# A hand-written order for the merge loop of a hybrid DiT block, with its sums on VectorE, and earlier sums in the first items of the up projection

## The chip, the cores and the metric

The kernel runs on one core of a Trainium2 chip. A core has five engines with queues of their own: TensorE (PE in the profile; its weight loads are shown apart as PEld), VectorE (DVE), ScalarE (ACT), GpSimd (POOL) and SyncE (SP), which here issues the loads and stores. Each engine works its own queue strictly in order; semaphores hold an instruction back until what it reads is there or what it overwrites has been read. The metric is the device time of one execution in microseconds.

## The reference

One layer on 1024 tokens of 1024 channels (batch 1), in fp32:

```python
attn = banded_window_attention(q, k, v, kc, vc, sink[l])
y = merge_branches(attn, fourier_mix(f), g_a, g_f, w_pa[l], w_pf[l], w_out[l])
x = x + gt1 * rmsnorm(y, g_post1[l])
h2 = modulate(rmsnorm(x, g_pre2[l]), sh2, sc2)
x = x + gt2 * rmsnorm(conv_ffn(h2, w_up[l], conv_w[l], conv_b[l], w_down[l]), g_post2[l])

def merge_branches(attn_o, four_o, g_a, g_f, w_pa, w_pf, w_out):
    m = jax.nn.sigmoid(g_a) * (attn_o @ w_pa) + jax.nn.sigmoid(g_f) * (four_o @ w_pf)
    return m @ w_out

def conv_ffn(h, w_up, conv_w, conv_b, w_down):
    u, gate = jnp.split(h @ w_up, 2, axis=-1)
    up = jnp.pad(u, ((0, 0), (1, 1), (0, 0)))
    u = up[:, :-2] * conv_w[0] + up[:, 1:-1] * conv_w[1] + up[:, 2:] * conv_w[2] + conv_b
    return (jax.nn.silu(u) * gate) @ w_down
```

## The kernel before

**Number format.** Each fp32 matrix is kept as two rounded parts, a high one (`h`, a cast on ScalarE, L80) and a low one (`l`, the value minus the high part, a subtraction at L68, which is the one line for all element-wise sums). A product is three matmuls, high·high, high·low, low·high, on three lines (L85, L86, L87; `mm3`).

**Merge.** The merged map is transposed, channels on partitions: 16 tiles of 128 channels (j = 0 to 7) by 512 tokens (h = 0, 1). A tile is 12 matmuls (4 K parts of 3) of `w_pa` (high `whpa`, low `wlpa`) with the attention's output (`ah`, `al`) into a PSUM bank `pa`; then `sga`, the gate's half, is multiplied by `pa` on DVE, `mf`, the Fourier half, gets `sga` added on POOL, and the sum is split into `mh` (ACT) and `ml` (DVE). The first two tiles are computed at the end of the attention (`EARLY`), the other 14 in a loop. The same loop loads and splits the four later blocks of `w_pa` (raw `wpa`; low part on POOL) and the 16 blocks of `w_out` (raw `wor`; parts `w0a`, `w0b` for the left half of the output channels, `woh` and `wol` for the right half; `wo_load`). Before the change this loop is plain code whose order on the engines is set by an automatic scheduler; in what follows it in the program, from the output map to the end, the order is the order of the code (`tc.manual_schedule()`). The tiles `sga` and `mf` of the sixth loop tile and later, and after them the rows `xr` of the residual, come from a pool `so` with 11 buffers that are handed on in order of allocation. The 8 DMA queue semaphores are used in turn, so each load of SP waits until the load eight before it has landed.

**Output map.** For 8 blocks of 128 tokens and two halves of the output channels, `y_mm(tk, h)` is 8 K parts of 3 matmuls, `mh` and `ml` being stationary. Then comes a token's chain: squares (`jy`, ACT), norm (a dozen small DVE operations, one square root on ACT), gate and residual (`z`, `xr`, DVE), squares, norm, scale (`z`), eight transposes on PE (`y_turn`, `ptz`, L160) and an affine step into `h` (`y_affine`, DVE and ACT).

**First items of the up projection.** It is a 2x2 Strassen product with seven products P1 to P7 for each of the row blocks j. Stationary operands are made from four blocks of `w_up` (`A_u`): A11, A12, A22 themselves and the sums S1 = A21+A22, S3 = A11−A21, S2 = S1−A11, S4 = A12−S2; each is then split (`conv`: `hP_u` on ACT, `lP_u` on DVE). Moving operands are made from `h`: B11, B21, B22 and T1, T2, T3, T4n, which are differences of quarters of the tokens (`t1` to `t4`), split by `hb_puts` (four casts of three quarters `a` and of one quarter `b` on ACT, and as many subtractions on DVE). The first items run in the order P1 (j = 0, 1, 2; `mm(0)` to `mm(2)`), P2 (j = 0, 1), P5 on T1 (`mm(5)` to `mm(7)`), P6 on T2 (`mm(8)` to `mm(10)`), P7 on T3 (`mm(11)` to `mm(13)`), then P4 of j = 0 on T4n (`mm(14)`) and P3 on B22; each is 12 matmuls. `evac` copies a bank to `snP_u` or adds it to a copy. From `run(14, M)` on, a planner goes through the items.

Of the kernel before, what the change touches and what calls it, by code (L numbers as in the profile page):

```python
# [16 lines left out]
P = 128  # L17
# [23 lines left out]
def block_kernel(ctx: ExitStack, tc: tile.TileContext, t: dict, out: bass.AP, dbg: dict):  # L41
# [169 lines left out]
    def wino(pairs, items, psf, hooks, slots=False, seng=None):  # L211
# [60 lines left out]
        def rest(j):  # L272
            if "P1" in st[j] and "S3" in st[j]:
                do_add(j, "S2")
                if "P2" in st[j]:
                    do_add(j, "S4")
# [1229 lines left out]
    for i in range(EARLY):  # L1506
        pa_tile(*PA[i], psB.tile([P, 1024], F, tag="ss", name=f"pa{i}", bufs=2)[:, :512])
# [27 lines left out]
    def wo_load(k, h):  # L1535
# [352 lines left out]
    with tc.manual_schedule():  # L1888
# [13 lines left out]

        def y_new(tk):
# [5 lines left out]

        xr_load(0)  # L1910
        for tk in range(6):
            xr_load(tk + 1)
            if tk:
                x1_store(tk - 1)
            if 1 <= tk < 4:
                pre(tk - 1, ("A11", "A21"))
            if 2 <= tk < 4:
                pre(tk - 2, ("A22",))
            y_mm(tk, 0)
            y_square(tk, 0)  # L1920
            y_mm(tk, 1, range(6))
            if tk:
                y_turn(tk - 1)
            y_mm(tk, 1, range(6, KT))
            if tk:
                y_affine(tk - 1, range(4), V)
                y_affine(tk - 1, range(4, 8), None)
# [8 lines left out]
            if 2 <= tk < 4:  # L1936
# [25 lines left out]
        pre(2, ("A12", "A22"))  # L1962
# [183 lines left out]
```

## Time and profile before

| | |
|---|---|
| Runs | 1362.89, 1367.26, 1368.34 us; median 1367.26 |
| Profiled execution | 1363.15 us; span 1361.4; granted clock 0.98 |
| Busy share of the span | PE 94%, PEld 76%, DVE 75%, ACT 51%, POOL 33% |
| DMA | 219.42 MB, mean 161 GB/s |
| Last matmul of the attention to the end of the first three tokens' output map | 528.85 to 614.97 us |
| Start of the up projection on PE | 672.94 us |

How to read it: in the trace PE is a single line of matmuls, so time is lost only where PE is idle or runs at a reduced clock. The profile's rows give a start, a duration, the engine, the line, the operation, the tiles and in brackets the idle time before with what ended it. The windows view gives, for a stretch of time, how long each engine was busy in it, and the clock that TensorE was granted (PEclk, 1.00 is full).

### The profile page before, as it was taken

To read this page: it belongs to the slowest core of one execution; us is meant where nothing else is said; L and a number is where in the kernel's file an instruction comes from. 1 tells how busy PE (TensorE), PEld (TensorE's weight loads), DVE (VectorE), ACT (ScalarE), POOL (GpSimd) and SP (SyncE) were. 2 spreads that over 40 slices of the span, in tenths; PEclk is the share of its full clock that TensorE was granted. 3 is DMA by queue.
4 is the path that set the end of the run, shared out by engine and by line. 5 is a ranking of instruction groups with operands and counts; after the bars stand their busy time and mean duration, and the time that the engine had idled before them with its cause. 6 is when DMAs were issued, how large, how long until landed. Compare 5 with 4: busy or idle time off the path is not lost.

```text
span 1361.4 us, 18457 instructions
## 1 busy us (share of the span) xinstructions
PE 1278.7 (94%) x5976; PEld 1031.9 (76%) x5976; DVE 1026.6 (75%) x1807; ACT 690.9 (51%) x1421; POOL 446.3 (33%) x337
## 2 busy tenths in 40 slices
PE   5889999999999999989989999999999988999896
PEld 3458777887878877778768788888888876878774
DVE  4787676974888985856689987766676687796987
ACT  5685346533667774434457554444454444543442
POOL 0000221200343343500004544454344355372764
PEclk9999999999999999899989999999999999999998
DMA  9986284614233436833203564444434559946563
GB/s 308 362 285 194 94 263 138 190 32 150 62 109 118 123 117 199 285 97 122 78 16 93 161 168 136 131 132 116 124 106 121 169 166 292 302 142 223 184 214 124
DMA packets 251125, 219.42 MB, mean 161 GB/s; under 512 B 14973, under 2 KB 204053, under 8 KB 251029
## 3 DMA queue, kind: packets, MB, share of 16 engines
q1 hardware_dynamic: 251028, 218.25, 52.2%
q8 instruction: 47, 0.77, 0.2%
q14 instruction: 50, 0.40, 0.1%
HBM read 159.20 MB, written 58.72 MB: 160 GB/s over the span
## 4 chain that ended last, share of the span: by engine, by line
PE 66%; DVE 14%; DMA 7%; issue 4%; ACT 3%; POOL 2%; SPq 2%; DVEq 0%; POOLq 0%; ACTq 0%
PE X_u L86 5%; PE X_u L87 5%; PE X_u L85 5%; PE Y_u L85 3%; PE Y_u L86 3%; PE Y_u L87 2%; PE y L87 2%; PE X_d L85 2%; PE y L85 2%; PE y L86 2%; DVE p L1285 2%; PE X_g L85 2%; PE X_d L87 2%; DVE pl L68 2%; PE X_d L86 2%
## 5 line engine op out<-in xcount | busy, mean ns | idle before, releaser
L68 DVE TENSOR_TENSOR lP_u<-A_u,hP_u 128x512 fp32r<-128x512 f32 x132 | 101.7, 779 | 48.3 <-ACT hP_u L303 46.5
L365 ACT COPY snP_u<-X_u 128x512 f32<-128x512 f32 x57 | 33.5, 588 | 138.2 <-PE X_u L87 130.4
L1305 POOL TENSOR_SCALAR p<-p,sm 128x640 f32<-128x640 f32 (+1 forms) x64 | 48.5, 778 | 84.3 <-PE po L1321 30.1
L68 POOL TENSOR_TENSOR yd<-yd,snP_d 128x512 f32<-128x512 f32 x36 | 52.2, 1451 | 70.2 <-ACT snP_d L365 70.2
L303 ACT CAST hP_u<-A_u 128x512 fp32r<-128x512 f32 x121 | 74.5, 619 | 0.1
L68 POOL TENSOR_TENSOR A_u<-A_u,A_u 128x512 f32<-128x512 f32 x39 | 62.9, 1613 | 34.3 <-DVE lP_u L68 21.0
L365 ACT COPY snP_d<-X_d 128x512 f32<-128x512 f32 x48 | 28.1, 586 | 78.7 <-PE X_d L87 78.7
L68 POOL TENSOR_TENSOR A_u<-S_u,A_u 128x512 f32<-128x512 f32 x19 | 24.9, 1309 | 104.1 <-DVE lP_u L68 104.1
L80 ACT CAST ph<-pp 128x512 fp32r<-128x512 f32 x76 | 44.3, 585 | 23.0 <-PE pp L1310 21.7
L68 DVE TENSOR_TENSOR pl<-pp,ph 128x512 fp32r<-128x512 f32 x76 | 51.7, 681 | 3.1 <-ACT ph L80 2.6
L1299 ACT ACTIVATE p<-p,nm 128x640 f32<-128x640 f32 (+1 forms) x64 | 51.3, 802 | 0.7 <-DVE nm L1292 0.7
L68 DVE TENSOR_TENSOR lP_d<-rP_d,hP_d 128x384 fp32r<-128x384 f32 x48 | 42.3, 882 | 10.5 <-ACT hP_d L303 10.3
L1285 DVE CUSTOM_DVE_ANT_0 p<-ss,mask 128x640 f32<-128x640 f32 (+1 forms) x64 | 49.9, 781 | 0.0
L1310 PE MATMUL pp<-ident,p 128*128 128x128 f32 x304 | 46.7, 274 | 3.2 <-POOL p L1305 1.8
L68 POOL TENSOR_TENSOR S_u<-A_u,A_u 128x512 f32<-128x512 f32 x19 | 34.5, 1816 | 39.5 <-DVE T4nb L68 38.9
L68 POOL TENSOR_TENSOR shk<-shk,rope 128x512 f32<-128x512 f32 x2 | 3.2, 1621 | 133.4 <-DMA A_g<-in_w_in 127.6
L1310 PEld LDWEIGHTS pp<-ident,p 128*128 128x128 f32 x304 | 37.2, 140 | 12.2 <-POOL p L1305 3.5
L1687 DVE SCALAR_TENSOR_TENSOR tb<-u,vec,tb 128x1024 f32<-128x1024 f32 x22 | 41.1, 1870 | 6.5 <-ACT tb L1684 6.5
L68 DVE TENSOR_TENSOR dB<-wd,dB 128x512 fp32r<-128x512 f32 x33 | 38.9, 1189 | 7.7 <-ACT dB L1758 7.7
L68 POOL TENSOR_TENSOR wd<-wd,wd 128x512 f32<-128x512 f32 x22 | 37.0, 1700 | 20.2 <-DVE dB L68 11.4
L68 DVE TENSOR_TENSOR u<-Y_u,snP_u 128x512 f32<-128x512 f32 x22 | 15.2, 690 | 37.3 <-PE Y_u L87 37.3
L68 POOL TENSOR_TENSOR fl<-fr,fh 128x512 fp32r<-128x512 f32 x6 | 7.6, 1286 | 100.0 <-ACT fh L80 99.1
(896 smaller groups left out, 4584.6 us busy)
## 6 DMA issues: line engine op xcount, KB each, us to landing
A_u<-in_w_up SPq DMA_DIRECT2D x88, 256.0 KB, 3.7
wd<-in_w_down SPq DMA_DIRECT2D x55, 256.0 KB, 4.5
wa<-in_w_mod SPq DMA_DIRECT2D x36, 256.0 KB, 5.3
A_g<-in_w_in SPq DMA_DIRECT2D x32, 256.0 KB, 5.3
ws<-in_w_mod SPq DMA_DIRECT2D x30, 256.0 KB, 6.0
wm<-in_w_mod SPq DMA_DIRECT2D x30, 256.0 KB, 4.6
bP_d<-g_d0P SPq DMA_DIRECT2D x56, 128.0 KB, 3.1
x<-in_x SPq DMA_DIRECT2D x16, 256.0 KB, 6.0
```

The lines of the kernel that those rows point to most:

```text
L68: return (eng or nc.vector).tensor_tensor(out=out, in0=a, in1=b, op=op)
L80: copy(hi, src)
L85: nc.tensor.matmul(ps, ah, bh, start=start, stop=False, skip_group_check=True)
L86: nc.tensor.matmul(ps, ah, bl, start=False, stop=False, skip_group_check=True)
L87: nc.tensor.matmul(ps, al, bh, start=False, stop=stop, skip_group_check=True)
L303: copy(st[j]["half", p][0], st[j][STA[p]])
L365: copy(d["s" + p], d["X"])
L1285: nc.vector.tensor_tensor_reduce(out=p_, in0=ssc[:, lo:768], in1=self.mk, op0=ALU.add, op1=ALU.max, scale=1.0, scalar=-3.0e38, accum_out=s ...
L1299: nc.scalar.activation(out=self.pt[g], in_=self.pt[g], func=AF.Exp, scale=SCALE, bias=self.m[:, g:g + 1], accum_out=self.sm[:, g:g + 1])
L1305: nc.gpsimd.tensor_scalar(out=self.pt[g], in0=self.pt[g], scalar1=self.sm[:, g:g + 1], scalar2=1.0, op0=ALU.mult, op1=ALU.mult)
L1310: nc.tensor.transpose(pp[:, g * P:(g + 1) * P], self.pt[g][:, j * P:(j + 1) * P], ident)
L1687: nc.vector.scalar_tensor_tensor(out=tb, in0=u[:, 0:1024], scalar=cw[0], in1=tb, op0=ALU.mult, op1=ALU.add)
```

## The change

It does five things.

1. The merge loop is written out in `merge(i)`, inside the part whose order is that of the code. `pa_tile` is cut into the matmuls (`pa_mm`), the product, sum and cast (`pa_out`) and the low part (`pa_low`). In one pass PE gets tile i; then come the loads of tile i+3's gates, one block of `w_out` with its cast, in four of the passes the load and the cast of a block of `w_pa`, `pa_out` of tile i−1, the low parts of the weight blocks, `pa_low` of tile i−1.
2. All 16 sums `mf` and the four low parts `wlpa` of the loop go from POOL to DVE. POOL has nothing in this stage then.
3. The right half's blocks of `w_out` are loaded after the loop, four before and four after the first matmuls of the output map. The map begins with tokens 0 and 1, left half, K parts 0 to 5 of both, then K parts 6 and 7 of both, then the right halves.
4. In tokens 3, 4 and 5, the sums S1, S3 and S2 of the row blocks 0, 1 and 2 are made right after the split for P1 (S3 and S2 were made behind T2's differences in the up projection); the same calls for block 2 further down then find them done. S4 is held back (`hold`). The blocks of `w_up` come one token later, A22 with them.
5. B21 is split right after B11, ahead of the right halves of tokens 6 and 7, and no longer behind them. The turn of token 7 goes from behind `mm(3)` to behind `mm(2)`, T1's differences and splits move with it, and most affine steps and evacuations of this part change places.

On DVE, from the end of the attention into the merge loop, the rows stand so before (`al` is the low part of the attention's output; `w0a`, `wlpa` and `ml` are the low parts named above):

```order
L68 TENSOR_TENSOR al_5785<-aT_3330,ah_5784 128x512
L68 TENSOR_TENSOR sga_5776<-pa_5889,sga_5776 128x512
L68 TENSOR_TENSOR ml_5905<-mf_5777,mh_5904 128x512
L68 TENSOR_TENSOR sga_5768<-pa_5837,sga_5768 128x512
L68 TENSOR_TENSOR sga_5772<-pa_5860,sga_5772 128x512
L68 TENSOR_TENSOR sga_5788<-pa_5912,sga_5788 128x512
L68 TENSOR_TENSOR sga_5942<-pa_5941,sga_5942 128x512
L68 TENSOR_TENSOR w0a_5817<-wor_5815,w0a_5817 128x512
```

and so after, in the same place:

```order
L68 TENSOR_TENSOR al_5785<-aT_3330,ah_5784 128x512
L68 TENSOR_TENSOR w0a_5874<-wor_5872,w0a_5874 128x512
L68 TENSOR_TENSOR sga_5768<-pa_5859,sga_5768 128x512
L68 TENSOR_TENSOR mf_5769<-mf_5769,sga_5768 128x512
L68 TENSOR_TENSOR w0a_5875<-wor_5901,w0a_5874 128x512
L68 TENSOR_TENSOR ml_5907<-mf_5769,mh_5906 128x512
L68 TENSOR_TENSOR sga_5772<-pa_5884,sga_5772 128x512
L68 TENSOR_TENSOR mf_5773<-mf_5773,sga_5772 128x512
L68 TENSOR_TENSOR w0a_5875<-wor_5928,w0a_5875 128x512
L68 TENSOR_TENSOR wlpa_5934<-wpa_5931,whpa_5933 128x512
L68 TENSOR_TENSOR ml_5939<-mf_5773,mh_5938 128x512
```

The low part of the first block of `w_out` now stands ahead of the first product `sga` of the loop, where five products stood ahead of it, and each tile has its sum `mf` and in two of the first four passes of the loop a block of `w_pa` on this engine.

On SP, around the twelfth allocation from the pool `so`, before (`wpa` and `wor` are raw weight blocks; mf_6084 is the twelfth):

```order
L1415 DMA sga_6083<-sga_d 128x512
L1559 DMA G_5804<-gt_d 128x512
L1559 DMA G_5805<-gt_d 128x512
L1415 DMA mf_6084<-mf_d 128x512
L1537 DMA wor_5856<-in_w_out 128x512
L1415 DMA sga_6112<-sga_d 128x512
L1537 DMA wor_5879<-in_w_out 128x512
L1335 DMA wpa_5883<-in_w_pa 128x4x128
```

and after (mf_6045 is the twelfth):

```order
L1545 DMA wor_6021<-in_w_out 128x512
L1415 DMA sga_6044<-sga_d 128x512
L1415 DMA mf_6045<-mf_d 128x512
L1545 DMA wor_6048<-in_w_out 128x512
L1335 DMA wpa_6051<-in_w_pa 128x4x128
L1415 DMA sga_6077<-sga_d 128x512
L1415 DMA mf_6078<-mf_d 128x512
L1545 DMA wor_6081<-in_w_out 128x512
```

The twelfth allocation goes into the buffer of the pool's first one; it stood four places ahead of a block of `w_pa` (the third of four) and stands two places ahead of it now. Before it needs a sum on POOL, after a sum on DVE.

On DVE in the up projection, from the last of T2's four differences `h` to the first split of T2, before (`S_u` and the `A_u` rows with an `A_u` or `S_u` at the left are the sums S1, S3, S2 and S4):

```order
L68 TENSOR_TENSOR h_6805<-h_7343,h_6805 128x512
L68 TENSOR_TENSOR A_u_6381<-A_u_6379,A_u_6381 128x512
L68 TENSOR_TENSOR A_u_6379<-S_u_6615,A_u_6379 128x512
L68 TENSOR_TENSOR A_u_6499<-A_u_6497,A_u_6499 128x512
L68 TENSOR_TENSOR A_u_6497<-S_u_6741,A_u_6497 128x512
L68 TENSOR_TENSOR A_u_6625<-A_u_6623,A_u_6625 128x512
L68 TENSOR_TENSOR A_u_6623<-S_u_7392,A_u_6623 128x512
L68 TENSOR_TENSOR lP_u_7429<-A_u_6379,hP_u_7428 128x512
L68 TENSOR_TENSOR A_u_6981<-A_u_6981,A_u_6379 128x512
L68 TENSOR_TENSOR u_7385<-Z_u_7344,snP_u_7400 128x512
L68 TENSOR_TENSOR T2a_7160<-h_6439,T2a_7159 128x3x128
```

and after, from the first of these differences:

```order
L68 TENSOR_TENSOR h_6502<-h_6920,h_6502 128x512
L68 TENSOR_TENSOR h_6549<-h_7052,h_6549 128x512
L68 TENSOR_TENSOR h_6669<-h_7265,h_6669 128x512
L68 TENSOR_TENSOR h_6797<-h_7321,h_6797 128x512
L68 TENSOR_TENSOR u_7390<-Z_u_7340,snP_u_7396 128x512
L68 TENSOR_TENSOR lP_u_7429<-A_u_6467,hP_u_7428 128x512
L68 TENSOR_TENSOR u_7393<-Z_u_7373,snP_u_7423 128x512
L68 TENSOR_TENSOR T2a_7186<-h_6502,T2a_7185 128x3x128
```

Six sums and one S4 have left this stretch; the six are made in tokens 3, 4 and 5, and the S4 behind the first split for P7.

The diff, cut to what the five points speak of:

```diff
@@ -272,7 +272,7 @@
         def rest(j):
             if "P1" in st[j] and "S3" in st[j]:
                 do_add(j, "S2")
-                if "P2" in st[j]:
+                if "P2" in st[j] and "hold" not in st[j]:
                     do_add(j, "S4")
@@ -1414,18 +1414,24 @@
-    def pa_tile(j, h, pp):
+    pap = {}
+
+    def pa_mm(j, h, pp):
         hi, lo = paw[j]
-        if (j, h) not in pal:
-            pa_load(j, h, so)
-        sg, mf = pal[j, h]
+        pap[j, h] = pp
         for k in range(4):
             mm3(pp, (hi[:, k * P:(k + 1) * P], lo[:, k * P:(k + 1) * P]), ah[k, h], k == 0, k == 3)
-        mul(sg, pp, sg)
-        add(mf, mf, sg, nc.gpsimd)
+
+    def pa_out(j, h):
+        sg, mf = pal[j, h]
+        mul(sg, pap[j, h], sg)
+        add(mf, mf, sg)
         alloc = (lambda n: s(n, R)) if j < 2 else (lambda n: o2(n, "ms", 24))
         msp[j, h] = (alloc(f"mh{j}{h}"), alloc(f"ml{j}{h}"))
-        split(*msp[j, h], mf)
+        copy(msp[j, h][0], mf)
+
+    def pa_low(j, h):
+        sub(msp[j, h][1], pal[j, h][1], fbits(msp[j, h][0]))
@@ -1543,14 +1551,29 @@
-        split(*wo[k, h], raw)
-
-    for i, (j, h) in enumerate(PA):
-        if i % 2 == 0 and 4 <= i // 2 + 4 < KT:
-            paw[i // 2 + 4] = merge_w(t["w_pa"], i // 2 + 4, "pa")
-        if i >= EARLY:
-            pa_tile(j, h, ps(f"pa{j}{h}"))
-        wo_load(i % KT, i // KT)
+        copy(wo[k, h][0], raw)
+        return lambda: sub(wo[k, h][1], raw, fbits(wo[k, h][0]))
+
+    def merge(i):
+
+        j, h = PA[i]
+        pa_mm(j, h, ps(f"pa{j}{h}"))
+        if i + 3 < len(PA) and PA[i + 3] not in pal:
+            pa_load(*PA[i + 3], so)
+        low = []
+        if i - EARLY < KT:
+            low.append(wo_load(i - EARLY, 0))
+        if i % 2 == 0 and 4 <= i // 2 + 2 < KT:
+            raw, m = merge_raw(t["w_pa"], i // 2 + 2, "pa"), i // 2 + 2
+            paw[m] = s(f"whpa{m}", R), s(f"wlpa{m}", R)
+            copy(paw[m][0], raw)
+            low.append(lambda: sub(paw[m][1], raw, fbits(paw[m][0])))
+        if i > EARLY:
+            pa_out(*PA[i - 1])
+        for f in low:
+            f()
+        if i > EARLY:
+            pa_low(*PA[i - 1])
@@ -1900,44 +1923,72 @@
-            if 2 <= tk < 5:
-                conv(tk - 2, "P1")
-            if 2 <= tk < 4:
-                sums(tk - 2, "S1")
-        xr_load(7)
...
+        for i in range(EARLY, len(PA)):
+            merge(i)
+        pa_out(*PA[-1])
+        low = [wo_load(k, 1) for k in range(4)]
+        for f in (lambda: pa_low(*PA[-1]), *low):
+            f()
+        xr_load(0)
+        xr_load(1)
+        for tk in range(2):
+            y_mm(tk, 0, range(6))
+        for tk in range(2):
+            y_mm(tk, 0, range(6, KT))
+        for f in [wo_load(k, 1) for k in range(4, KT)]:
+            f()
+        for tk in range(2):
+            y_square(tk, 0)
+        y_mm(0, 1)
+        y_token(0)
+        y_mm(1, 1)
+        y_token(1)
+        for tk in range(2, 6):
...
+            if 2 < tk:
+                conv(tk - 3, "P1")
+                sums(tk - 3, "S1")
+                sums(tk - 3, "S3")
+                sums(tk - 3, "S2")
...
         for j in range(2):
+            st[j]["hold"] = True
             pre(j, ("A12",))
@@ -1949,8 +2000,13 @@
         hb_puts(hb, "B11", {c: h2[c, 0] for c in range(4)})
+        hb_puts(hb, "B21", {c: h2[c, 1] for c in range(4)})
         y_mm(6, 1)
         y_square(6, 1)
+        conv(2, "P1")
+        sums(2, "S1")
+        sums(2, "S3")
+        sums(2, "S2")
         y_norm(6, (0,))
@@ -1959,38 +2015,41 @@
-        pre(2, ("A12", "A22"))
-        hb_puts(hb, "B21", {c: h2[c, 1] for c in range(4)})
         y_square(7, 1)
         mm(0)
...
-        mm(2)
-        y_affine(6, range(4, 8), None)
+        hb_puts(hb, "T1", {0: h2[0, 0], 1: h2[1, 0]})
+        y_affine(7, (0, 1), V)
+        y_affine(7, (2, 3), None)
         t1(2)
-        hb_puts(hb, "T1", {0: h2[0, 0], 1: h2[1, 0]})
+        t1(3)
         mm(3)
-        y_turn(7)
-        mm(4)
...
         hb_puts(hb, "T1", {2: h2[2, 0], 3: h2[3, 0]})
         conv(0, "P5")
+        y_affine(6, range(4, 8), None)
         y_affine(7, range(4, 8), None)
+        mm(4)
@@ -1998,18 +2057,15 @@
+        evac(0)
         conv(1, "P5")
-        sums(2, "S1")
         conv(2, "P5")
-        for j in range(3):
-            evac(j)
         mm(5)
-        evac(3)
         for c in range(4):
             t2(c)
-        for j in range(3):
-            sums(j, "S3")
-            sums(j, "S2")
+        evac(1)
+        evac(2)
+        evac(3)
         conv(0, "P6")
         mm(6)
```

More of the change, by code (lines that the diff above doesn't have):

```diff
@@ L1506, in block_kernel @@
     for i in range(EARLY):
-        pa_tile(*PA[i], psB.tile([P, 1024], F, tag="ss", name=f"pa{i}", bufs=2)[:, :512])
+        pa_mm(*PA[i], psB.tile([P, 1024], F, tag="ss", name=f"pa{i}", bufs=2)[:, :512])
+        pa_out(*PA[i])
+        pa_low(*PA[i])
     for jh in PA[2:5]:
@@ L1901, in t4, with y_token @@
             sub(h2[c, 0], h2[c, 1], h2[c, 0])
-        def y_new(tk):
-            for h in range(2):
-                y_gate(tk, h)
-                y_res(tk, h, V)
-                x_sq(tk, h)
[L1910 to L1916, printed above, removed]
-            if 2 <= tk < 4:
[L1918 to L1927, printed above, removed]
+        def y_token(tk):
             y_square(tk, 1)
@@ L1968, in block_kernel @@
         z_scale(6, 1)
-        y_new(7)
+        for h in range(2):
+            y_gate(7, h)
+            y_res(7, h, V)
+        x_sq(7, 0)
         mm(1, range(2))
@@ L2027, in block_kernel @@
         for j in range(3):
+            st[j].pop("hold", None)
             conv(j, "P7")
```

43 lines of the change are left out of this document (35 added, 8 removed).

## The prediction

> **What bounds the kernel now.** I began with the page's busy shares, went to the windows view of the stretch that the change touches, then to the list of waits of TensorE there, and last to the timeline of the engine each wait names.
>
> ```profile
> PE 1278.7 (94%) x5976; PEld 1031.9 (76%) x5976; DVE 1026.6 (75%) x1807; ACT 690.9 (51%) x1421; POOL 446.3 (33%) x337
> ```
>
> TensorE is busy 94% of the span, so only its idle or slowed time can be won. The windows (engine, busy us, instructions; then granted clock, DMA share, GB/s):
>
> ```profile
> 529.08:614.90 85.82, 78.20 (x329) 62.92 (x328) 55.78 (x101) 33.30 (x70) 25.98 (x18) 0.94 0.66 214
> 614.90:672.94 58.04, 58.04 (x275) 48.40 (x273) 38.68 (x120) 24.64 (x76) 0.00 (x0) 1.00 0.28 91
> 672.94:731.50 58.56, 48.87 (x198) 38.60 (x197) 49.42 (x113) 38.69 (x101) 6.63 (x6) 0.88 0.20 61
> 731.50:771.30 39.80, 38.06 (x169) 31.17 (x167) 38.45 (x38) 22.25 (x34) 23.06 (x14) 1.00 0.29 82
> 771.30:1100.00 328.70, 328.70 (x1450) 272.27 (x1451) 231.87 (x280) 156.39 (x257) 149.25 (x103) 1.00 0.49 138
> ```
>
> The merge (first row) and the first up items (third) are the leaky stretches: TensorE idles 7.6 and 9.7 us, at clocks of 0.94 and 0.88. The tokens between have no idle time. In the fourth row VectorE is busy 38.45 of 39.80 us, so it hands a delay on; behind it TensorE is full again, and what is won by 771 stays won. The waits of TensorE, first from 500 to 600, then from 600 to 770 us:
>
> ```profile
> PE pa L85 <- ACT whpa L80: 3.0, 1, 3.0
> PE y L87 <- DVE ml L68: 2.6, 1, 2.6
> PE y L85 <- ACT mh L80: 1.3, 1, 1.3
> PE pa L86 <- DVE al L68: 0.7, 1, 0.7
> ...
> PE ptz L160 <- ACT z L1617: 3.3, 1, 3.3
> PE X_u L86 <- DVE T2a L68: 3.2, 1, 3.2
> PE X_u L85 <- ACT T2a L80: 2.6, 1, 2.6
> PE Y_u L85 <- ACT hP_u L80: 0.6, 1, 0.6
> ```
>
> Each wait costs more than itself where the clock then drops:
>
> ```profile
> 555.69 0.39 PE L87 MATMUL pa<-ah,wlpa 128*128 128x512 f32 x1
> 557.05 0.39 PE L87 MATMUL pa<-ah,wlpa 128*128 128x512 f32 x1
> 560.42 0.80 PE L85 MATMUL pa<-ah,whpa 128*128 128x512 f32 x1 [2.98 <-ACT whpa L80]
> 561.44 0.63 PE L85 MATMUL pa<-ah,whpa 128*128 128x512 f32 x1
> 561.87 0.63 PE L86 MATMUL pa<-al,whpa 128*128 128x512 f32 x1
> 584.10 0.80 PE L87 MATMUL y<-w0b,ml 128*128 128x512 f32 x1 [2.63 <-DVE ml L68]
> ```
>
> From 555.69 to 557.05 six matmuls start 0.227 us apart; after the wait of 2.98 us the pitch is 0.43 us for a while. The 312 matmuls of the first window would take 312 x 0.227 = 70.8 us, with about 1.6 us of transposes 72.4; it lasts 85.8, so 13.4 us are lost there.
>
> **The merge loop.** Its queues:
>
> ```profile
> 532.86 1.29 DVE L68 TENSOR_TENSOR al<-aT,ah 128x512 fp32r<-128x512 f32 x2
> 543.76 2.47 DVE L68 TENSOR_TENSOR sga<-pa,sga 128x512 f32<-128x512 f32 x4
> 544.57 5.49 POOL L68 TENSOR_TENSOR mf<-mf,sga 128x512 f32<-128x512 f32 x4 [1.28 <-issue]
> L68 DVE TENSOR_TENSOR ml<-mf,mh x16: 676/892/1777, 531.6 to 584.2; 128x512 fp32r<-128x512 f32 x16
> 538.25 0.32 SPq L1415 DMA_DIRECT2D mf<-mf_d  x1
> 542.56 0.38 SPq L1335 DMA_DIRECT2D wpa<-in_w_pa  x1
> 550.09 0.32 SPq L1415 DMA_DIRECT2D mf<-mf_d  x1
> A_u<-in_w_up SPq DMA_DIRECT2D x88, 256.0 KB, 3.7
> ```
>
> (The fourth row gives least, median and longest in ns.) Four products on VectorE took 2.47 us, 0.62 each, and two subtractions with POOL idle 1.29. The sum on POOL took 5.49/4 = 1.37. With POOL still I price VectorE's operations at 0.60 to 0.65, 0.72 where one waits for the last, and not at the median 0.89 of `ml`.
>
> - *Start.* Two sums in the attention's tail stand ahead of `pl` and `po`: 0.65 us later (0 to 1.3). Tile (0,1) now runs all K parts at once and must wait for the last `al`, done at 534.15 + 0.65; before, other tiles' first parts filled this. Cost 2.1 us (1.5 to 2.5).
> - *VectorE falls behind.* The first product now stands behind the low part of the first `w_out` block, the eleventh load. The load at 542.56 waits for that load to land (eight before it), so it lands at about 542.5; with a cast of 0.62 and the subtraction VectorE starts the loop at about 543.9, when TensorE has finished that tile at 535.3. The lag, nearly 9 us, stays: 54 operations (14 each of `sga`, `mf`, `ml`, 8 of `w_out`, 4 of `wlpa`) make 2.5 to 3.1 us a tile, 39 us in all, against 2.72 (12 x 0.227) on TensorE.
> - *The pool of 11.* The twelfth `so` tile waited before for a sum on POOL that ended at 550.06, and was issued at 550.09. Now it waits for the sum of tile 6 on the lagging VectorE: 543.9 + 5 tiles = about 557.8, where the queue alone would issue it at 550.7. The third late `wpa` block stands two loads behind: issued at 558.7, landed after 3.7 us (the median of the same shape), cast; TensorE has it at 563.05 against 560.85 when it needs it. That is 2.2 us, 0.3 of ramp and 1.6 to 3.2 us of reduced clock. The first two late blocks cost 0.6 and 0.45 by their low parts, the fourth about 2 us on VectorE.
> - *End.* VectorE's 39 us and 5.5 us of waits end its last `ml` at about 588.4. The K-part order gives TensorE 36 matmuls (8.2 us) meanwhile, so the `ml` wait of before (2.63) shrinks, but the right half starts at 589.1. After token 0's chain (an estimate of 9.6 us from its steps, which makes one turn 1.4 late) token 2's right half ends at 613.7 against 614.97: **1.2 us won**. If the pool wait bites less (the block arrives in time) it is 5.3; if two blocks take 5.4 us to land, the median of the window 536 to 575, it is −2.2.
>
> ```profile
> wpa<-in_w_pa SPq DMA_DIRECT2D x3, 256.0 KB, 5.4
> ```
>
> The Trainium skill, page "TensorE: Matmul & The Clock Gate", section "What's actually happening", gives half rate only after an idle window of about 3.4 us, free-running. By that the 2.2-us wait would cost no clock, and the merge would win up to 3.2 us more. The trace disagrees: waits of 2.98 and 2.63 us were both followed by the 0.43 pitch.
>
> **Tokens 2 to 5.** Three more sums a token (2.0 us) on VectorE, which is busy 38.68 of 58.04 us; a token is 48 matmuls and its transposes on TensorE, 11.7 us, against 7.8 + 2.0 on VectorE (38.68 over the 4.96 tokens of that row). The cover is TensorE's own work: 0, at worst 1 us.
>
> **Up projection.** The rows on which the shift rests:
>
> ```profile
> 673.66 1.74 ACT L80 CAST B21a<-h 128x384 fp32r<-128x384 f32 x4
> 676.10 0.59 ACT L1569 ACTIVATE jy<-y 128x512 f32<-128x512 f32 x1
> 680.44 1.97 PE L160 MATMUL ptz<-ident,z 128*128 128x128 f32 x8 [3.26 <-ACT z L1617]
> 690.95 1.04 PE L160 MATMUL ptz<-ident,z 128*128 128x128 f32 x8
> 695.39 0.50 PE L85 MATMUL Y_u<-T1a,hP_u 128*128 128x512 f32 x1 [0.65 <-ACT hP_u L80]
> 702.89 0.68 DVE L68 TENSOR_TENSOR A_u<-A_u,A_u 128x512 f32<-128x512 f32 x1
> 706.26 0.69 DVE L68 TENSOR_TENSOR A_u<-S_u,A_u 128x512 f32<-128x512 f32 x1
> 706.73 0.80 PE L85 MATMUL X_u<-T2a,hP_u 128*128 128x512 f32 x1 [2.60 <-ACT T2a L80]
> 710.68 0.79 PE L86 MATMUL X_u<-T2a,hP_u 128*128 128x512 f32 x1 [3.15 <-DVE T2a L68]
> 728.14 0.68 DVE L68 TENSOR_TENSOR lP_u<-A_u,hP_u 128x512 fp32r<-128x512 f32 x1
> ```
>
> - *B21 sooner.* Its casts (from 673.66) held the squares `jy` until 676.10, though TensorE had left that bank at 672.94. Without them `jy` runs at 674.3 and `z` is ready 1.1 to 1.7 us sooner: the wait of 3.26 becomes 1.57, perhaps without the clock drop. The same casts in front of token 6's norm cost 0.4 us there, hidden by 5.4 us of token 7's matmuls.
> - *Turn 7 sooner* (684.6 to 685.4 for 690.95) lets T1's second half be ready for `mm(5)` at 691.2 to 691.9, against 695.39; `mm(7)` ends at 700.8 instead of 703.97, with 0.9 us for a cast behind affine steps on ScalarE.
> - *Sums away.* From 702.89 to the end of the sixth, 706.95, six sums stood ahead of T2's split. Without them and with the rest sooner, `mm(8)` waits 1.4 us for the low part of T2 and not 2.60 + 3.15 (and a drop), and ends at 704.9, 9.7 us sooner than before.
> - *What is late next.* `mm(14)` reuses a bank whose copy now stands behind B22's casts, and its stationary low part stands behind S4 and all the splits: about 720.0 and 721.05, a wait of 2.1. VectorE does this low part at 721.0 instead of 728.14, so it is 7.1 to 7.8 us ahead and carries that through the window in which it paces. **7.5 us won** (4.4, if two more such waits with drops open, to 9.7).
>
> Sum: 1.2 + 7.5 = 8.7 us. The profiled execution took 1363.15 us (span 1361.4 and 1.75 around it), 4.1 below the median of the three runs, 1367.26. That gives 1354.5 from the one and 1358.6 from the other; I take 1356.5.
>
> **Rivals.**
> - *The pool wait does not bite.* If VectorE starts the loop sooner than 543.9, or the twelfth load is not what the weight waits for, the merge wins 5.3: 12.8 in all, 1350.3 from the profile. For it: the wait is only 2.2 us against a chain of many estimates. Against: the row at 550.09 shows the ring at work.
> - *VectorE becomes the bound of the merge: slower.* 54 operations at the median 0.89 of the `ml` row instead of 0.60 take 54 x 0.29 = 15.7 us more, and TensorE, which needs every `ml`, gets them all: 8.7 won turns into 7.0 lost, 1370.2. It decides from an excess of 8.7/54 = 0.16 us an operation. For it: VectorE has no slack, at 39 us against 38 on TensorE. Against: the two subtractions in 1.29 us at 532.86, with POOL idle; the long ones lie beside POOL's sums. The Trainium skill, page "Perfetto Trace Analysis", section "Optimizing Scalar/DVE Operations", holds that with a saturated VectorE moving work off it, even to GpSimd, may pay, which speaks against this change; it adds that the two share a port, for which the slow `ml` beside POOL are evidence.
> - *The up projection gives it back.* If `mm(14)` and the planner's items behind it wait for VectorE's backlog, only 2 to 4 us stay, with 1.2 of the merge: about 1361 from the middle of my two bases. For it: VectorE is busy 49.42 of 58.56 us there before, and 38.45 of 39.80 behind. Against: the sums that left are 4.1 us of that load, and their cover in the tokens is real.
>
> **How the numbers follow.** Forecast (6 to 11 us won) 0.50; no pool wait 0.20; given back 0.20; slower 0.10. A change of 0.5%, 6.8 us, is about what three runs that spread over 5.5 us can tell. Faster by more: 0.38 of the forecast's half, all of the second and 0.02 of the third, 0.60; slower by more, 0.07 of the last; 0.33 lies between. The range runs from 1348, a little under the second case, to 1365, beyond the third; what lies outside is the last case and the far ends.
>
> **What would show it.** Right: POOL empty from 529 to 614; the first `sga` on VectorE at 543 to 544, behind `w0a`; `mf` loads that wait for VectorE near 557; TensorE waiting for `whpa` of the tile before the last four near 561; the turn of token 6 with a wait under 2 us; T2 starting within 1.5 us of T1's last matmul; a new wait before T4n. Wrong: VectorE's mean in the merge above 0.75 us, TensorE idle in tokens 2 to 5, or a start of the up projection (672.94 before) that is later.

## The result

The changed kernel takes 1354.36 us (median of 4 runs, 1352.74 to 1356.86) against 1366.7 us (4 runs, 1362.89 to 1368.34): a ratio of 0.9915, 95% interval [0.9888, 0.9942], which is 11.6 us of 1366.7 with an interval of 7.9 to 15.3. The forecast was 1356.5 in a range from 1348 to 1365.

The windows view of the changed kernel, over the same five stretches (engine, busy us, instructions; then granted clock, DMA share, GB/s):

```profile
529.08:614.90 85.82, 78.69 (x338) 62.15 (x337) 59.20 (x119) 34.51 (x73) 1.29 (x1) 0.98 0.59 194
614.90:672.94 58.04, 58.04 (x274) 48.38 (x273) 46.08 (x137) 26.98 (x83) 0.00 (x0) 1.00 0.40 123
672.94:731.50 58.56, 54.50 (x239) 42.53 (x238) 51.25 (x107) 42.34 (x101) 13.73 (x10) 1.00 0.22 66
731.50:771.30 39.80, 38.07 (x168) 31.19 (x168) 38.55 (x41) 21.68 (x34) 20.67 (x13) 1.00 0.49 137
771.30:1100.00 328.70, 328.70 (x1452) 272.18 (x1451) 231.52 (x275) 156.17 (x257) 154.36 (x105) 1.00 0.48 135
```

In the third row TensorE is busy 54.50 us in place of 48.87, at full clock in place of 0.88: the up projection has lost most of its holes. In the first row its busy time has hardly moved (78.69 for 78.20), although GpSimd is now idle. The tokens between are as full as before. TensorE's waits from 500 to 600 and from 600 to 770 us say the same:

```profile
PE pa L85 <- ACT whpa L1569: 3.2, 2, 1.8
PE pa L86 <- DVE al L68: 1.5, 2, 0.8
...
PE Y_u L85 <- DVE gg L68: 1.7, 1, 1.7
PE X_u L86 <- DVE T2a L68: 1.2, 1, 1.2
PE ptz L160 <- ACT z L1640: 1.0, 1, 1.0
...
PE X_u L85 <- ACT snP_u L293: 0.9, 1, 0.9
PE Y_u L85 <- ACT hP_u L80: 0.5, 1, 0.5
PE X_u L87 <- DVE lP_u L68: 0.4, 1, 0.4
```

The waits for T2, 5.75 us before, are 1.2; the 3.3 for token 6's turn is 1.0. In the merge the waits for `ml` and `mh` (3.9 us) are gone, those for `whpa` have stayed (3.0 us before, 3.2 now), and short ones for `al`, `ah`, `woh` and `wol` have come.

Three landmarks divide the profiled execution: the first matmul of the merge, the end of token 2's output map (the first matmul of token 3), and the start of the up projection. The wait for `gg` closes the stretch in which VectorE paces.

```profile
530.75 0.39 PE L85 MATMUL pa<-ah,whpa 128*128 128x512 f32 x1
614.86 0.39 PE L85 MATMUL y<-w0a,mh 128*128 128x512 f32 x1
672.87 0.39 PE L85 MATMUL X_u<-B11a,hP_u 128*128 128x512 f32 x1
762.01 0.50 PE L85 MATMUL Y_u<-B22a,hP_u 128*128 128x512 f32 x1 [1.73 <-DVE gg L68]
```

| stretch, us | before | changed | won |
|---|---|---|---|
| merge: first matmul to token 2's end | 85.89 | 84.11 | 1.8 |
| tokens 3 to 7 | 57.97 | 58.01 | 0.0 |
| up: its start to the wait for `gg` | 98.36 | 89.14 | 9.2 |

(Before: 529.08, 614.97, 672.94 and 771.30.) Each row is one execution: in three more kernels below with the same merge code the first row takes 83.1 to 84.3 us, and 85.6 in another execution of the merge of before, so the 1.8 stands for 1.3 to 2.8. These are 11.0 us. The spans differ only by 7.7, because two things outside the change ran against the changed kernel in this one execution: it was 1.5 us later when it came to the merge, and it lost 1.6 us near 1311 to a clock drop that the other execution did not have. The last section shows that drop. So the two stretches are compared below rather than single spans; "merge" and "up" always mean the first and the third row of this table, and the ratios of the kernels are each to the kernel before, measured in the same session.

### The profile page after: what moved, and what is told of

It is laid out like the page before. It is cut to its first block, busy times and chain, and to the rows that moved or that the text cites. A ratio compares the mean times of both kernels' runs of the same rounds, so it can differ in the third digit from the quotient of the medians.

```text
span 1353.7 us, 18460 instructions
## 1 busy us (share of the span) xinstructions
PE 1276.7 (94%) x5976; PEld 1027.9 (76%) x5976; DVE 1028.8 (76%) x1827; ACT 691.2 (51%) x1421; POOL 418.6 (31%) x317
## 4 chain that ended last, share of the span: by engine, by line
PE 64%; DVE 20%; ACT 5%; DMA 5%; issue 4%; POOL 1%; SPq 0%; DVEq 0%; POOLq 0%; ACTq 0%
PE X_u L87 5%; PE X_u L85 5%; PE X_u L86 5%; PE Y_u L85 2%; PE Y_u L87 2%; PE Y_u L86 2%; PE X_g L85 2%; PE X_g L87 2%; PE X_g L86 2%; DVE p L1285 2%; PE X_d L85 2%; PE X_d L86 2%; PE X_d L87 2%; DVE pl L68 2%; DVE dT L68 2%
```

## The experiments

### Each half alone

One kernel has the new merge and first tokens, with the up projection as before:

```diff
             if 2 < tk:
                 conv(tk - 3, "P1")
+            if 2 < tk < 5:
                 sums(tk - 3, "S1")
-                sums(tk - 3, "S3")
-                sums(tk - 3, "S2")
...
-            st[j]["hold"] = True
...
```

From there to `run(14, M)` it has the text of the kernel before.

> The new merge loop, its sums on VectorE and the K parts of the first two tokens, with the up projection as before (B21 behind token 7, sums behind T2's differences, turn 7 behind mm(3)). Theory A (the change pays in the up projection, about 9 us, and the merge stage gives under 2): 1 to 2.5 us below before, about 1364.5; token 2 ends within 0.5 us of where the changed kernel has it (614.9), and the wait for the last gg before the full stretch stands near 771, as before. Theory B (the merge is worth half): 5 us or more below before, about 1361.

Measured: 1363.29 us, ratio to before 0.9989 [0.9979, 0.9998], so 1.5 us. Merge 83.2, up 96.8. The time is where theory A put it; its two landmarks are not. Token 2 ends at 612.8: this execution came to the merge 1.1 us sooner, and its merge is 0.9 shorter. The wait for `gg` stands at 767.6: the up projection starts 2.1 us sooner, and with the code of before it takes 1.6 us less than in the profile of before. What differs is a clock drop: token 6's turn waits 3.12 us here and 3.26 there, but its eight transposes take 1.27 us here and 1.97 there, and only there do the matmuls behind them run at a pitch of 0.43 us.

The other has the scheduler's merge with its sums on GpSimd and the rest as changed:

```diff
-        for i in range(EARLY, len(PA)):
-            merge(i)
...
+        y_mm(0, 0)
+        y_square(0, 0)
+        y_mm(0, 1)
+        y_token(0)
```

The loop of the kernel before stands outside the ordered part again.

> The merge loop as before, ordered by the scheduler with its sums on POOL, and the first two tokens without K parts; tokens 2 to 7 and the up projection as changed. Theory A: about 9 us below before, 1357.5, with the wait for gg 9 us sooner after the start of the up projection (89 us behind it, not 98). Theory B: about 5 below, 1361.5.

Measured: 1354.94 us, ratio 0.9925 [0.9908, 0.9942], so 10.2 us. Merge 85.6, up 89.05. That is the 89 us of theory A. The halves add up to the whole (0.9989 x 0.9925 = 0.9914): almost all of the gain comes from the up projection.

### What in the up projection pays

```diff
                 sums(tk - 3, "S1")
-                sums(tk - 3, "S3")
-                sums(tk - 3, "S2")
...
         for c in range(4):
             t2(c)
+        for j in range(3):
+            sums(j, "S3")
+            sums(j, "S2")
```

> The changed kernel with the sums S3 and S2 back behind T2's differences, S1 of block 2 with them and S4 no longer held back. If the sums' place is what TensorE paid for: six sums of 0.66 us stand again ahead of T2's split, the wait for T2's low part goes from 1.18 to about 5 us with a stretch at half clock, and the kernel is 4 to 6 us slower than the changed one, 1358.5 to 1360.5. If VectorE paces this stretch by its total work wherever it is put (rival): the six sums cost their 4 us of VectorE and nothing at the wait for T4n, 1 to 4 us slower. If they were covered: under 1 us.

Measured: 1360.64 us, 0.9967 [0.9954, 0.998]; up 95.4, that is 6.2 us more than the changed kernel's 89.1. The rows of TensorE at T2 (bracket: idle time before and what ended it):

```profile
703.23 0.51 PE L85 MATMUL X_u<-T2a,hP_u 128*128 128x512 f32 x1 [2.90 <-ACT T2a L80]
707.79 0.80 PE L86 MATMUL X_u<-T2a,hP_u 128*128 128x512 f32 x1 [4.05 <-DVE T2a L68]
```

6.95 us of waits in place of 1.18, and a matmul of 0.80 us, the sign of the reduced clock. The place of the sums (seven here, with block 2's S1) is worth 6.2 us, a little over the 4 to 6 expected and more than the 1 to 4 of the rival; that they were covered is refuted. That VectorE paces this stretch is not, as the table below shows.

```diff
-        hb_puts(hb, "B21", {c: h2[c, 1] for c in range(4)})
         y_mm(6, 1)
...
         x1_store(6)
+        hb_puts(hb, "B21", {c: h2[c, 1] for c in range(4)})
         y_square(7, 1)
```

> The changed kernel with the split of B21 back behind token 7's last matmuls; everything else, turn 7 behind mm(2) too, stays. If the early turns hang on the squares that stood behind these casts: the wait of turn 6 goes from 1.02 to about 3 us, every item to mm(8) is 2 to 3 us later, and the kernel 2 to 3.5 us slower than the changed one, about 1357. If VectorE's queue sets the end of this stretch and not the turns (rival): the wait is longer, but the wait for T2 takes it up, and the time stays within 1 us of the changed one.

Measured: 1356.78 us, 0.9937 [0.9922, 0.9952]; up 91.2, 2.05 more than the changed kernel.

```profile
677.21 1.27 PE L160 MATMUL ptz<-ident,z 128*128 128x128 f32 x8 [3.12 <-ACT z L1640]
700.21 0.50 PE L86 MATMUL X_u<-T2a,hP_u 128*128 128x512 f32 x1 [1.19 <-DVE T2a L68]
```

The turn's wait is 3.12 us for 1.02, and the wait at T2 is unchanged (1.19 for 1.18): the delay goes through to the end and nothing takes it up. But the edit also puts B21's subtractions back into this stretch of VectorE. VectorE's time from the start of the up projection to the wait for `gg`, from the windows view:

| kernel | up, us | VectorE busy | VectorE idle |
|---|---|---|---|
| before | 98.36 | 87.87 | 10.49 |
| new merge alone | 96.76 | 87.77 | 8.99 |
| changed | 89.14 | 80.58 | 8.56 |
| sums late | 95.38 | 85.24 | 10.14 |
| B21 late | 91.19 | 82.86 | 8.33 |

Of the 9.2 us, 7.3 are work that VectorE no longer does between these two points, but earlier, and 1.9 are idle time. With the sums late it is busy 4.7 us more and idle 1.6 more; with B21 late it is busy 2.3 more and idle 0.2 less. So both edits cost about what they put back on VectorE. Whether B21 costs its 2.05 us by the later turn or by its subtractions on VectorE, the two being of the same size, this run cannot tell. The two effects (6.2 and 2.05) make 8.3 of the 9.2 against the profile of before; against the new merge alone, without that clock drop, the up half is worth 7.7 in all. What turn 7 sooner adds no run took apart.

### What holds the merge

The forecast had put the rest of the merge's loss on VectorE's late start and, through the pool of 11, on late weights. A first edit put cast and low part of each `w_out` block one pass later and behind the tile's product, sum and cast, and the cast of a `w_pa` block behind them too:

```diff
...
+        return lambda: (copy(wo[k, h][0], raw), sub(wo[k, h][1], raw, fbits(wo[k, h][0])))
...
-        low = []
+        low = list(late_wo)
+        late_wo.clear()
         if i - EARLY < KT:
-            low.append(wo_load(i - EARLY, 0))
+            late_wo.append(wo_load(i - EARLY, 0))
...
-            copy(paw[m][0], raw)
-            low.append(lambda: sub(paw[m][1], raw, fbits(paw[m][0])))
+            low.append(lambda: (copy(paw[m][0], raw), sub(paw[m][1], raw, fbits(paw[m][0]))))
         if i > EARLY:
             pa_out(*PA[i - 1])
         for f in low:
             f()
```

> The changed kernel with the splits of the left half's w_out blocks one pass later and behind the tile's product, sum and cast, so that the first product of the merge loop no longer stands behind the first w_out block. The stage is measured from the first matmul of the merge to the end of token 2's output map: 85.9 us before, 84.1 in the changed kernel, 83.1 to 84.3 in the other kernels with its merge loop. Theory (VectorE's late start of nearly 9 us, through the pool of 11, makes the late weights late): VectorE starts the loop at 538 to 540 and not at 545, the twelfth allocation is loaded near 553, TensorE no longer waits for whpa (3.2 us), stage 80 to 81, kernel 3 to 4 us below the changed one, 1350.5. Rival (the weights are late because the loads in front of them fill the queue): waits for whpa stay over 2 us, stage 83 to 84.

Measured: 1358.13 us, 0.9941 [0.992, 0.9962]; merge 87.2, 3 us longer than the changed kernel's. Both theories missed, and VectorE's rows tell why:

```profile
537.50 0.69 DVE L68 TENSOR_TENSOR sga<-pa,sga 128x512 f32<-128x512 f32 x1 [1.51 <-PE pa L87]
545.42 0.69 DVE L68 TENSOR_TENSOR w0a<-wor,w0a 128x512 fp32r<-128x512 f32 x1 [6.45 <-ACT w0a L1557]
549.25 0.69 DVE L68 TENSOR_TENSOR w0a<-wor,w0a 128x512 fp32r<-128x512 f32 x1 [1.21 <-ACT w0a L1557]
```

The first product runs at 537.50, about as expected, but the first tile's `ml` still stands behind the first block of `w_out`, which lands no sooner. And with the block's cast behind the tile's cast on ScalarE, VectorE waits 1.2 us for it in each further pass with such a block. In the changed kernel the low part of `w_out` fills the time in which ScalarE casts `mh`: VectorE waits for `mh`, 0.69 us a tile, only in the last six passes, which have no weight block. The twelfth allocation is loaded at 561.3, not near 553, and TensorE's waits for `whpa` grow from 3.2 to 4.3 us.

The next kernel loads each late block of `w_pa` one pass sooner, ahead of that pass's gates; a third has both edits:

```diff
+        if i % 2 and 4 <= (i + 5) // 2 < KT:
+            praw[(i + 5) // 2] = merge_raw(t["w_pa"], (i + 5) // 2, "pa")
         if i + 3 < len(PA) and PA[i + 3] not in pal:
             pa_load(*PA[i + 3], so)
```

> The changed kernel with each late block of w_pa loaded one pass sooner, ahead of that pass's gates, so that it does not stand behind the twelfth allocation of the pool of 11. VectorE's late start stays. Theory: TensorE's waits for whpa go to under 0.5 us, but VectorE's lag of 9 us stays and its last ml ends 1 to 2.5 us sooner, so the stage is 81.5 to 83. Rival (those waits were all that held the stage): 80 or less.

> Both of the two edits of the runs beside it: w_out's splits behind the product and a pass later, w_pa's late blocks a pass sooner. If late start and pool are one cause, this adds little to the first: stage 80 to 81. If they add: stage 78 to 79.5, kernel about 1349.

Measured: 1352.47 us, 0.9902 [0.988, 0.9924], merge 83.8; and 1357.12 us, 0.9945 [0.9925, 0.9965], merge 86.9. The first alone moves TensorE's two waits for `whpa` to other tiles (550 and 565, 3.4 us together): at 564.04 the block's cast stands behind that of a `w_out` block for which ScalarE waited 3.50 us, and which the pool of 11 holds up. The waits did not go, so the run cannot say what the stage would be without them, and neither expectation came about. VectorE starts 1.8 us later, since the first `w_out` block now lands behind a `w_pa` block, but no longer waits for `wlpa` (2.7 us in the changed kernel). The run with both edits has the fault of the first edit (VectorE waits 1.2 us for the cast in the passes with a `w_out` block) and says nothing more.

```diff
-        add(mf, mf, sg)
+        add(mf, mf, sg, nc.gpsimd)
...
-            low.append(lambda: sub(paw[m][1], raw, fbits(paw[m][0])))
+            low.append(lambda: sub(paw[m][1], raw, fbits(paw[m][0]), nc.gpsimd))
```

> The changed kernel, in its order by hand, with the 16 sums mf and the four late low parts wlpa on GpSimd again. Theory (the sum stands between product and cast in one chain, and in an order by hand VectorE waits for it at ml): a sum of 1.4 us and two hand-overs in place of 0.72 make 3.5 us a tile without other work, VectorE's last ml is 5 to 10 us later, stage 88 to 93. Rival (VectorE had no slack, so what leaves it wins): stage under 83.

Measured: 1364.53 us, 1.0003 [0.999, 1.0016]; merge 94.8. The waits of VectorE in the loop, from 537 to 600 us:

```profile
DVE ml L68 <- ACT mh L1431: 25.9, 13, 3.5
DVE w0a L68 <- ACT w0a L1554: 9.6, 2, 9.0
...
```

In this order by hand the sum on GpSimd makes VectorE wait 25.9 us at `ml` (13 waits, 2 us each), against 4.1 us (6 waits) with the sums on VectorE. The merge is 10.7 us longer than the changed kernel's (94.8, where 88 to 93 was expected); TensorE's 5.1 us of waits for `wlpa`, also on GpSimd here, are part of this kernel. But the scheduler's merge of before, with the same sums on GpSimd, is only 1.5 to 1.8 longer than the changed one (85.6 to 85.9): its order ran several products ahead of their sums. The sums' engine and the order go together.

```diff
         for tk in range(2):
-            y_mm(tk, 0, range(6))
-        for tk in range(2):
-            y_mm(tk, 0, range(6, KT))
+            y_mm(tk, 0)
```

> The changed kernel with the left halves of tokens 0 and 1 computed one after the other over all eight K parts. Theory (the K parts cover VectorE's lag, which is about 9 us at the end of the loop): TensorE waits 3 to 4 us for the parts of tile (7,0) after about 4 us of token 0, with a clock drop perhaps, and the stage from the first matmul of the merge to the turn of token 1 is 84.8 to 86.5 in place of 81.8; kernel 3 to 4.5 us slower than the changed one. Rival (the chain of VectorE and token 0's norm set the end, whatever TensorE does first): under 1 us.

Measured: 1358.92 us, 0.9951 [0.9935, 0.9966]; from the first matmul of the merge to token 1's turn 85.3 us for 81.8, as expected. By the ratios the kernel is 4.9 us slower, a little beyond the 3 to 4.5.

```profile
584.89 0.79 PE L85 MATMUL y<-w0b,mh 128*128 128x512 f32 x1 [3.35 <-ACT mh L1431]
```

The wait of 3.35 us is the lag that the K parts cover.

### A version that beats both

The loads stay where they are, but a block is split only three passes (`w_out`) or two passes (`w_pa`) later, its cast still ahead of the tile's product:

```diff
...
         if i - EARLY < KT:
-            low.append(wo_load(i - EARLY, 0))
+            late.setdefault(i + 3, []).append(wo_load(i - EARLY, 0))
...
+            late.setdefault(i + 2, []).append((paw[m][0], paw[m][1], raw))
+        low = late.pop(i, [])
+        for hi, _, raw in low:
+            copy(hi, raw)
         if i > EARLY:
             pa_out(*PA[i - 1])
+        for hi, lo, raw in low:
+            sub(lo, raw, fbits(hi))
         if i > EARLY:
             pa_low(*PA[i - 1])
```

> The changed kernel with the loads where they are, but the splits of w_out's left half three passes later and those of the late w_pa blocks two passes later, each cast still ahead of the tile's product, so that neither ScalarE nor VectorE stands waiting for a block that has not landed. (The run that put the casts behind the tile's product only moved the wait and lengthened VectorE's period to 3.8 and 4.4 us a tile.) Theory (the stage is set by VectorE's chain, which starts at 544.5, 7 us after its first product could run): first product near 537.5, last ml at 577 to 580 and not 588.8, the twelfth allocation loaded by 552, no wait for whpa over 0.5 us, first matmul of the merge to the turn of token 1 76 to 78.5 in place of 81.8, kernel 3 to 6 us below the changed one, about 1350. Rival (loads and TensorE's own start set it): 80.5 or more.

Measured: 1347.55 us (1346.92 to 1349.15), 0.9868 [0.9851, 0.9885] of before, against 0.9915 for the changed kernel. Its first window and its waits of TensorE from 526 to 616 us:

```profile
529.08:614.90 85.82, 82.34 (x364) 66.11 (x363) 63.21 (x132) 36.46 (x79) 1.27 (x1) 1.00 0.65 212
```

```profile
PE pa L86 <- DVE al L68: 1.5, 2, 0.8
PE ptz L160 <- DVE z L1647: 1.0, 1, 1.0
PE pa L85 <- ACT ah L80: 0.7, 1, 0.7
```

No wait for `whpa` is left, and the clock in this window is full. The rows of VectorE and SP that the theory named:

```profile
536.55 0.69 DVE L68 TENSOR_TENSOR sga<-pa,sga 128x512 f32<-128x512 f32 x1 [0.92 <-PE pa L87]
578.50 0.69 DVE L68 TENSOR_TENSOR ml<-mf,mh 128x512 fp32r<-128x512 f32 x1 [0.69 <-ACT mh L1431]
552.19 0.32 SPq L1415 DMA_DIRECT2D mf<-mf_d  x1
```

The first product runs at 536.6, the last `ml` at 578.5, the twelfth allocation is loaded at 552.2. Merge 78.1 (84.1 in the changed kernel), to token 1's turn 75.7, a little better than expected.

This edit removes VectorE's late start and TensorE's waits for `whpa` together. Which of them had held the stage can be read from all the kernels with this order, by when VectorE's last `ml` ends (us from the first matmul of the merge):

| kernel | TensorE's waits for `w_pa` | last `ml` ends | merge | from `ml` to the end |
|---|---|---|---|---|
| changed | 3.2 | 58.75 | 84.11 | 25.36 |
| new merge alone | 2.3 | 57.80 | 83.17 | 25.37 |
| sums late | 2.9 | 58.89 | 84.28 | 25.39 |
| B21 late | 2.0 | 57.72 | 83.08 | 25.36 |
| `w_out` behind | 4.3 | 61.81 | 87.19 | 25.38 |
| `w_pa` first | 3.9 | 58.41 | 83.79 | 25.38 |
| both | 5.3 | 61.51 | 86.90 | 25.39 |
| sums on GpSimd | 8.1 | 69.49 | 94.82 | 25.33 |
| splits later | 0 | 48.63 | 78.06 | 29.43 |

(Waits for `whpa` and `wlpa`. The kernel without the K parts has another order behind the loop and is left out.) In eight kernels the stage ends 25.3 to 25.4 us after the last `ml`, whatever TensorE waited before. So VectorE's chain set the stage in the changed kernel, and splits that waited for blocks not yet landed had delayed it: 8.7 us at the first `w_out` block, and 4.8 us at three later blocks (2.1 for one of `w_out`, 2.7 for two of `w_pa`). With the splits later the last `ml` comes 10.1 us sooner and the merge is only 6.0 shorter: VectorE is no longer the last there, and TensorE waits only 3.2 us in all up to token 1's turn, against 7.1 in the changed kernel.

The run beside it also puts the copy and the stationary split of `mm(14)` between T4n's and B22's casts:

```diff
         hb_puts(hb, "T4n", {c: h2[c, 0] for c in range(4)})
+        ahead(11)
+        evac(11)
         hb_puts(hb, "B22", {c: h2[c + 4, 1] for c in range(4)})
-        for k in range(11, 14):
+        for k in range(12, 14):
```

> The run beside it, with the stationary split of P4 and the copy of the bank that mm(14) reuses put between the casts of T4n and B22. The two waits ahead of mm(14), 0.90 and 0.44 us, go. Theory (from 690 to the wait for gg near 762 VectorE paces, and its work is the same): the start of the up projection to the wait for gg stays at 89.1 within 0.3, no gain. Rival (these waits are the last that TensorE loses there): 1 to 1.3 us less, 87.9.

Measured: 1349.85 us, 0.9888 [0.9872, 0.9904]; up 89.4 for 89.1. The waits have only moved to B22:

```profile
715.58 0.50 PE L86 MATMUL Y_u<-B22a,hP_u 128*128 128x512 f32 x1 [0.53 <-DVE B22a L68]
716.99 0.50 PE L87 MATMUL Y_u<-B22a,lP_u 128*128 128x512 f32 x1 [0.91 <-DVE lP_u L68]
756.84 0.50 PE L85 MATMUL Y_u<-B22a,hP_u 128*128 128x512 f32 x1 [1.93 <-DVE gg L68]
```

VectorE paces up to `gg` (busy 81.07 of 89.42 us), and a wait that TensorE loses there comes back at the next one. The median is 2.3 us above that of the run beside it; the spans of the two profiles differ by 0.4, so what makes the rest stays open.

## Why the prediction was right

The direction, the two places and the likeliest time held; the two terms were 1.2 + 7.5 = 8.7 us against 1.6 + 9.2 = 10.8, where the 1.6 is the merge's 1.8 less a start that is 0.2 later. The time came out 2.1 us below the likeliest one, and the gain is 2.9 larger than forecast (11.6 for 8.7). The base taken, 1365.2, lies 1.5 below the median of before, 1366.7, which brought the two times closer: that part is luck.

- **Tail and start.** Two sums in the attention's tail: predicted 0.65; the merge starts 35.80 us after the last common wait near 494, 35.59 before, so 0.2. The first two tiles of the loop waited 0.70 + 0.72 + 0.78 = 2.2 us (predicted 2.1), of which the first 0.70 stood before as well.
- **VectorE's late start.** The row that the forecast asked for is there, with `w0a` ahead:

```profile
544.49 0.69 DVE L68 TENSOR_TENSOR w0a<-wor,w0a 128x512 fp32r<-128x512 f32 x1 [8.67 <-ACT w0a L1554]
545.22 0.69 DVE L68 TENSOR_TENSOR sga<-pa,sga 128x512 f32<-128x512 f32 x1
588.81 0.69 DVE L68 TENSOR_TENSOR ml<-mf,mh 128x512 fp32r<-128x512 f32 x1 [0.69 <-ACT mh L1431]
```

  The first product came 14.5 us after the merge's first matmul (predicted 14.8), the last `ml` ended at 589.5 (588.4, with a start 1.7 sooner). From the first `w0a` to there the chain took 45.0 us, with 44.5 predicted (39 of work, 5.5 of waits). The 54 operations took 0.69 us each and followed each other at 0.60 to 0.72: the price with GpSimd idle was right, and the slower rival's price of 0.89 is refuted. That VectorE's chain would end the stage was in the forecast itself, which counts the end from the last `ml`, and the table above bears it out.
- **The pool of 11.** It bites where it was put:

```profile
550.80 0.32 SPq L1415 DMA_DIRECT2D sga<-sga_d  x1
558.46 0.32 SPq L1415 DMA_DIRECT2D mf<-mf_d  x1
559.35 0.38 SPq L1335 DMA_DIRECT2D wpa<-in_w_pa  x1
564.16 0.50 PE L85 MATMUL pa<-ah,whpa 128*128 128x512 f32 x1 [1.35 <-ACT whpa L1569]
571.99 0.50 PE L85 MATMUL pa<-ah,whpa 128*128 128x512 f32 x1 [1.82 <-ACT whpa L1569]
```

  SP stands for 7.7 us before the twelfth allocation, issued at 558.46 (predicted 557.8). TensorE's waits were 1.35 and 1.82, in place of 2.2 and of 2 on VectorE alone, and the reduced clock expected behind them (1.6 to 3.2 us) did not come; a drop came at 536.5 to 539.5 instead, behind the three short waits of the start. Neither is lost time of itself, since the stage ends with VectorE's last `ml`. What the pool costs is what the late blocks make VectorE wait, at most 4.8 us here.
- **Tokens 2 to 5** cost nothing, as the second window shows: TensorE busy 58.04 of 58.04 us.
- **Up projection.** `mm(5)` began at 689.93 (predicted 691.2 to 691.9, before 695.39), T2's low part made TensorE wait 1.18 (1.4). The term that was too small is "what is late next": a wait of 2.1 us ahead of `mm(14)`, and 7.1 to 7.8 us for VectorE. Measured:

```profile
718.47 0.50 PE L85 MATMUL X_u<-T4na,hP_u 128*128 128x512 f32 x1 [0.90 <-ACT snP_u L293]
719.64 0.50 PE L87 MATMUL X_u<-T4na,lP_u 128*128 128x512 f32 x1 [0.44 <-DVE lP_u L68]
718.89 0.69 DVE L68 TENSOR_TENSOR lP_u<-A_u,hP_u 128x512 fp32r<-128x512 f32 x1
```

  1.34 us of waits, and VectorE at this operation at 718.89 in place of 728.14: 9.25 sooner, and the wait for `gg` then comes 9.29 sooner. The step was right that VectorE's lead is what is carried; its size was short by 1.7. How much of that is the forecast's is open: 1.6 of the 9.2 are the clock drop in the profile of before, and the runs with the up half alone give 10.2 us, with 7.9 to 12.6 by their interval.
- **The rule against the change** (the Trainium skill, page "Perfetto Trace Analysis", section "Optimizing Scalar/DVE Operations": off a saturated VectorE, even to GpSimd, may make sense, though between these two it might not help) would have misled here in its first half: with these sums on GpSimd, in this order, the merge is 10.7 us longer. What counted was the chain from product to `ml`, with 25.9 us of waits at `ml`, not VectorE's total.

## What to carry to other kernels

Where an engine works its queue in order, look at what stands ahead of the first instruction of a loop: one weight block that lands late, put there for neatness, moved a whole chain by more than 8 us, and splitting it and the blocks behind it two or three passes later won 6 us. Work that fills an engine's time between two dependent steps must have its own input ready by then, or it is a wait in disguise. A sum moved out of a stretch that an engine paces into one that it does not is worth its full time, and may be worth more if the hole had slowed the clock. To see which engine ends a stage, measure in several kernels from its last operation to the end: if that stays the same while the rest changes, it is this engine's chain.

## What the hardware showed

The same wait can cost nothing or 1.6 us. In the down projection, whose code is the same in both kernels, TensorE waits 2.17 us in the kernel before and 2.16 in the changed one (first row of before, then four of the changed kernel):

```profile
1319.02 0.50 PE L85 MATMUL Y_d<-dB,hP_d 128*128 128x512 f32 x1 [2.17 <-DVE yd L68]
```

```profile
1309.84 0.50 PE L85 MATMUL Y_d<-dB,hP_d 128*128 128x512 f32 x1 [2.16 <-DVE yd L68]
1311.12 0.39 PE L87 MATMUL Y_d<-dB,lP_d 128*128 128x512 f32 x1
1311.35 0.59 PE L85 MATMUL Y_d<-dB,hP_d 128*128 128x512 f32 x1
1314.72 0.43 PE L87 MATMUL X_d<-dT,lP_d 128*128 128x512 f32 x1
```

Before, the matmuls behind the wait run at the full pitch of 0.23 us. In the changed kernel they start at full speed and slow down 1.5 us later, from 1311.35 to 1314.72, 3.4 us: eight matmuls at 0.43 us, 1.6 us lost. A hundred us earlier it is the other way round, behind a wait of 1.81 us in the kernel before and of 1.83 in the changed one (three rows of before, then two of the changed kernel):

```profile
1214.82 0.50 PE L85 MATMUL X_d<-dT,hP_d 128*128 128x512 f32 x1 [1.81 <-ACT snP_d L365]
1217.12 0.63 PE L85 MATMUL X_d<-dT,hP_d 128*128 128x512 f32 x1
1225.87 0.50 PE L85 MATMUL Y_d<-dB,hP_d 128*128 128x512 f32 x1 [0.97 <-DVE yd L68]
```

```profile
1205.64 0.50 PE L85 MATMUL X_d<-dT,hP_d 128*128 128x512 f32 x1 [1.83 <-ACT snP_d L365]
1216.69 0.50 PE L85 MATMUL Y_d<-dB,hP_d 128*128 128x512 f32 x1 [2.58 <-DVE yd L68]
```

Before, the clock drops from 1215.4 to 1218.4, yet the next item starts 11.05 us after the wait in both: the drop has only shortened the next wait, from 2.58 us to 0.97. It cost nothing here: TensorE waits for VectorE next in both.

The late drop fits what the Trainium skill, page "TensorE: Matmul & The Clock Gate", section "What's actually happening", says of a window of 3413 ns that runs free of the program. It does not fit the section's idle time of about 3.4 us as the condition: 2.16 and 1.81 were enough here, while 2.17 and 1.83 in the other kernel and 1.82 in the merge were followed by no drop. That the phase of such a window decides which waits are hit is a reading that no run here tested. Single profiles of the same code differ by a few us, and the stretches above carry the argument.
